# Attention stage of a hybrid decoder: the queries are projected first, projections run four steps further ahead, stored outputs return one transfer per step, the values' staging gets a second buffer, and chunk copies are placed behind the tiles turned on TensorE

## The chip, the cores and the metric

One Trainium2 chip, one of its NeuronCores. A core has five engines with a queue of instructions each, which meet only through semaphores: TensorE (PE, with weight loads shown apart as PEld), VectorE (DVE), ScalarE (ACT), GpSimd (POOL) and SyncE (SP), and 16 DMA engines that the queues of SP and POOL feed here. The metric is the device time of one execution in microseconds (us); several executions are summed up by their median.

## The reference

The whole trunk is one program: a recurrent layer, an attention layer, a dense feed-forward network behind each, with an RMS norm ahead of every part. The change touches the attention layer alone: 1024 positions, 16 heads of 64, causal, and instead of a softmax each weight is a share of what the later positions have left over.

```python
def stick_breaking_attention(x, w_qkv, w_o):
    qkv = jnp.einsum("bsd,de->bse", x, w_qkv).reshape(bsz, seq, 3, N_HEADS, HEAD_DIM)
    ...
        z = jnp.einsum("bhqd,bhkd->bhqk", qb, kb).astype(jnp.float32) * scale
        log_fail = jnp.where(strict, jax.nn.log_sigmoid(-z), 0.0)
        suffix = lax.cumsum(log_fail, axis=3, reverse=True) - log_fail
        weights = jnp.where(strict, jnp.exp(jax.nn.log_sigmoid(z) + suffix), 0.0)
        outs.append(jnp.einsum("bhqk,bhkd->bhqd", weights.astype(vb.dtype), vb))
    ...
    return jnp.einsum("bse,ed->bsd", o, w_o)
```

## The kernel before

Numbers that enter a matmul are split into a high and a low part, and a product is three matmuls (high by high, high by low, low by high: lines 143 to 145). Attention takes the 16 heads as eight pairs `q` = 0 to 7, each with two heads `hx`.

**Projections.** `qkv_steps(q)` projects queries, keys and values of a pair from the layer's input `xh`, `xl` (eight slices of 128 features, two halves `n` of 512 positions). One of its steps is three matmuls, one of its six groups (a projection of one half) is eight steps. After a group `evacuate` takes the result out of PSUM: queries and keys into `two` (high and low), from which `spread` sends them by DMA on POOL's queue into the tiles `q` (four transfers of 128 KB a half) and `kk` (four of 256 KB); values into `t` and from there, in two tasks a step apart, into `vx` (high by ACT, low by DVE), which two DMA transposes on SP's queue turn into `v`. `vx` has one buffer before. Of pair 0 the order is queries, keys, values, and of later pairs keys, queries, values (`kind`).

**The main loop.** It runs over steps `u`. A step computes the scores of one chunk (128 queries by up to 512 keys, `z_part`, L1682 and L1683), puts them through a sigmoid (ACT, L1695) and a running product (DVE, `scan`, L1702 and L1705), multiplies one finished tile of weights by the values (`av_part`, L1750), does two steps of projections (`fill`), one task of the list `later` and the tasks of the list `soon` that are due. 24 steps make a pair. Chunks run ten steps ahead of the multiplication by the values. The projections stand further ahead by `AHEAD` of their own steps.

**Two ways to turn weights.** Before they meet the values, weights must have keys on the partitions. Chunks on the diagonal are turned by PE itself (`t_part`, L1727), copied as `th` (ACT) and `tl` (DVE) by `t_split`. The four chunks of a head off the diagonal go through `turn_weights`: `wx` (high by ACT, L1712, low by DVE, L1713, three buffers) and a DMA transpose on SP's queue, `wt<-wx`. `av_part` reads `wt` at the steps with a remainder of 8 to 11 (first head) and 20 to 23 (second head) by 24; the four transposes of the first head are issued at steps -1 to 2, those of the second at 11 to 14. In a step, the copy of the chunk before stands ahead of `t_split`.

**Outputs.** A pair's output is added up by `gather`, `add_v` (L1766, on POOL, for pair 7 on DVE) and `parts`. The outputs of pairs 0 to 5 and the first half of pair 6 can't stay on the chip, since `xh` and `xl` are still read; `store` sends them to DRAM (`odh`, `odl`, 256 KB each), and when the last values are projected `bring_back` loads them into `xh` and `xl`, whose tiles bear names of earlier use in the profile (`vh`, `vl`, `xg`). There are 26 such transfers on POOL's queue, 12 issued at step 163 and 14 at step 168. `out_fill` puts the first matmuls of the output projection (`ob`) into the last steps; `amount` lists how many at which step, counted from 168.

The lists `soon` and `later` and the loop itself write the order of every engine's queue; nothing is reordered afterwards. A tile with several buffers waits, when it is written again, for the last readers of the buffer.

Of the kernel before, what the change touches and what calls it, by code (L numbers as in the profile page):

```python
# [10 lines left out]
BF16 = mybir.dt.bfloat16  # L11
F16 = mybir.dt.float16
# [5 lines left out]
P = 128  # L18
S = 1024
D = 1024  # L20
# [14 lines left out]
def trunk(  # L35
# [93 lines left out]
    def cols(w, c0, n=P):  # L129
        return w[:, c0 : c0 + n].rearrange("(k p) c -> p k c", p=P)  # L130
# [1357 lines left out]
    with ExitStack() as st:  # L1488
# [21 lines left out]
        later, soon, raws, sv, av_ = [], [], {}, {}, {}  # L1510

        def bring_back(*which):
            for q, n in which:
                nc.gpsimd.dma_start(f32(xh[q][n]), od[q, n][0])
                nc.gpsimd.dma_start(f32(xl[q][n]), od[q, n][1])


        def kind(q, i):
            return i if q == 0 else (1, 0, 2)[i]

        def stage(task, steps=1):
            soon.append([steps, task])

        def load_link(i):
            q, which = divmod(i, 3)
            if q < NP:
                raws[i] = load_raw(cols(w_qkv, kind(q, which) * D + q * P), (ND,))
            else:
                mix[0].load(which)

        def column_norms(raw, q):
            sq = ap.tile([P, ND, P], BF16, tag="sq", name="sq", bufs=1)
            r3 = raw.rearrange("p (k c) -> p k c", k=ND)
# [38 lines left out]
        def qkv_steps(q):  # L1572
            for which in range(3):
# [12 lines left out]
                for n in range(NH):  # L1586
                    pool, tag = (psZ, "z") if (q, which) == (0, 0) else (psQ, "qk")
                    ps = pool.tile([P, NB], F32, tag=tag, name="qk_ps")
                    for i, k in enumerate(ks):
                        mm3(ps, w[0][:, k], w[1][:, k], xh[k][n], xl[k][n], i == 0, i == ND - 1)  # L1590
                        if i < ND - 1:
                            yield
                    ev = evacuate(q, kind(q, which), n, ps)
                    next(ev)
# [4 lines left out]
        def evacuate(q, which, n, ps):  # L1599
            full = lambda tag, m: [ap.tile([P, m, S], F32R, tag=tag, name=tag, bufs=4 if m == 1 else 3) for _ in range(2)]  # L1600
            cs = slice(n * NB, (n + 1) * NB)
            if which == 2:
# [6 lines left out]
                nc.vector.scalar_tensor_tensor(after, ps, f32(sv[q]), rbc[n], op0=ALU.mult, op1=ALU.mult)  # L1609
                yield  # L1610
                nc.vector.tensor_sub(t, VT[q][:, cs], after)
                vx = ap.tile([P, 4, 2, P], F16, tag="vx", name="vx", bufs=1)
                t3 = t.rearrange("p (b c) -> p b c", b=4)

                def low():
# [3 lines left out]
                    for hx, a in enumerate((top, bot)):  # L1619
# [4 lines left out]
                        )  # L1624
                    if q == NP - 1:
                        back = [(p, n) for p in range(NP - 2)]
                        stage(lambda: bring_back(*([(NP - 2, 0)] * n + back)), 1 + n)

                def high():
# [112 lines left out]
        def av_part(tht, q, hx, G, kb, first, last):  # L1742
# [21 lines left out]
            def add_v():  # L1764
                eng = nc.vector if q == NP - 1 else nc.gpsimd
                eng.tensor_add(oo[q, G], oo[q, G], VT[q][:, G * NB + 1 : (G + 1) * NB + 1])  # L1766
# [27 lines left out]
        units = [u for q, hx in heads for u in unit_list(q, hx)]  # L1794
        LEAD, AHEAD = 10, 4

# [26 lines left out]
        with tc.manual_schedule(engines={E.PE, E.Activation, E.DVE, E.Pool, E.SP}):  # L1823
# [30 lines left out]
            last_two, out_work = len(units) - 2 * 12, out_fill()  # L1854
            amount = {x: 2 for x in (-1, 0, 1, 9, 10, 11, 12)}
            amount.update({x: 1 for x in range(14, 21)})
            c = 0
            for u in range(-LEAD, len(units)):
                some = chunks[c : c + 1]
                c += 1  # L1860
                if u < -2:
                    for _ in range(2):
                        next(fill, None)
                due()
                for a in some:
                    z_rest(z_part(*a), *a)
                    if u % 2 or u < -2:
                        scan(*a)
                while turning:
                    turn_weights(*turning.pop(0))  # L1870
                for a in some:
                    if not a[-1]:
                        turning.append(a)
                if u % 2 == 0 and u >= 0:
                    av_part(ready.pop(u, None), *units[u])
                if u % 2 == 0 and 0 <= u + 2 < len(units):
                    two = {x: t_part(*units[x]) for x in (u + 2, u + 3) if x % 12 < 8}
                    for x, tp in two.items():
                        ready[x] = t_split(tp, *units[x])
                if u % 2 == 0 and u >= -2:  # L1880
                    for a in some:
                        scan(*a)
# [67 lines left out]
```

## Time and profile before

| what | value |
|---|---|
| time, median of 3 runs | 2190.91 us (2189.57 to 2195.8) |
| the profiled execution | 2187.32 us, its span 2185.5 us |
| granted TensorE clock, mean | 0.992 |
| busy of the span: PE, DVE, ACT, POOL | 98%, 81%, 52%, 11% |
| attention stage | from about 955 to 1465 us of the span |
| wt<-wx transposes | 64, median 4.3 us from issue to landing |

The profile lists instructions by line, engine and tiles (out<-in, buffer numbers left out). "Idle before" is the time that an engine stood still ahead of an instruction, and the name behind it is what ended last of what it waited for. A wait names only the last link: where ACT keeps PE waiting, ACT's own waits must be looked up.

### The profile page before, as it was taken

Reading aid. Unit: us, or ns where it says so; the run is one execution under the profiler, and the core shown is the slowest. Engines: PE = TensorE matmul, PEld = TensorE weight load, DVE = VectorE, ACT = ScalarE, POOL = GpSimd, SP = SyncE. Lnnn points to the kernel's source line nnn. Section 1 sums busy time; section 2 is a strip of 40 time slices with the busy share of each in tenths; the row PEclk is TensorE's granted clock in tenths of the full one; section 3 lists DMA queues with packets and bytes.
Section 4 is the critical chain, followed back from the end, with each engine's and each line's share of the span. In section 5 each row is a group of like instructions: output and inputs, shape, how many; then the busy total and the mean of one; then the engine's idle time right before and its main releaser. Section 6 shows DMA issues by size and latency. Waiting matters only on the chain.

```text
span 2185.5 us, 28142 instructions
## 1 busy us (share of the span) xinstructions
PE 2132.9 (98%) x10158; PEld 1743.8 (80%) x10158; DVE 1780.7 (81%) x2607; ACT 1130.6 (52%) x1838; POOL 233.7 (11%) x282
## 2 busy tenths in 40 slices
PE   8999999999999999999999999779999999999998
PEld 7888888888888888887777777558888888888887
DVE  7888778888888887877888888766888888888886
ACT  6577445444444544655565565443544444454556
POOL 1222020000000000012223322411000000000002
PEclk9999999999999999999999999889999999999999
DMA  7111422344446864446777766984133444587452
GB/s 233 49 49 39 164 89 71 102 136 149 145 157 201 275 206 122 147 141 126 146 154 147 145 134 136 206 180 133 56 105 120 154 144 151 170 277 238 138 152 92
DMA packets 380843, 315.46 MB, mean 144 GB/s; under 512 B 101272, under 2 KB 296992, under 8 KB 380704
## 3 DMA queue, kind: packets, MB, share of 16 engines
q1 hardware_dynamic: 368192, 274.60, 42.7%
q0 software_dynamic: 12352, 38.81, 7.9%
q8 instruction: 79, 1.29, 0.2%
q14 instruction: 60, 0.49, 0.1%
q10 hardware_dynamic: 160, 0.27, 0.0%
HBM read 184.09 MB, written 83.36 MB: 122 GB/s over the span
## 4 chain that ended last, share of the span: by engine, by line
PE 86%; DMA 5%; DVE 5%; ACT 2%; issue 2%; SPq 0%; DVEq 0%; ACTq 0%
PE p_ps L143 17%; PE p_ps L144 17%; PE p_ps L145 17%; DMA wt<-wx 3%; PE a_ps L144 3%; PE a_ps L145 3%; PE a_ps L143 3%; PE ob_ps L143 2%; PE ob_ps L145 2%; PE ob_ps L144 2%; PE qk_ps L143 2%; PE qk_ps L145 2%; PE qk_ps L144 2%; PE av_ps L1750 2%; DMA v<-vx 2%
## 5 line engine op out<-in xcount | busy, mean ns | idle before, releaser
L143 PE MATMUL p_ps<-vh,wbh 128*128 128x512 f32 x524 | 204.9, 391 | 0.0
L144 PE MATMUL p_ps<-vl,wbh 128*128 128x512 f32 x524 | 204.5, 390 | 0.0
L145 PE MATMUL p_ps<-vh,wbl 128*128 128x512 f32 x524 | 204.0, 389 | 0.2 <-DVE wbl L726 0.2
L143 PE MATMUL p_ps<-vh,wch 128*128 128x512 f32 x524 | 204.1, 390 | 0.0
L145 PE MATMUL p_ps<-vh,wcl 128*128 128x512 f32 x524 | 204.1, 389 | 0.0
L144 PE MATMUL p_ps<-vl,wch 128*128 128x512 f32 x524 | 203.9, 389 | 0.0
L722 ACT CAST wbh<-sb 128x1024 fp32r<-128x1024 f32 (+2 forms) x69 | 69.6, 1009 | 192.6 <-DVE sb L702 192.6
L1695 ACT ACTIVATE w<-z_ps,rs 128x128 f32<-128x128 f32 (+1 forms) x192 | 111.1, 581 | 94.9 <-PE z_ps L1683 93.6
L145 PE MATMUL p_ps<-vh,wal 128*128 128x512 f32 x396 | 154.1, 389 | 0.0
L143 PE MATMUL p_ps<-vh,wah 128*128 128x512 f32 x396 | 154.0, 389 | 0.0
L144 PE MATMUL p_ps<-vl,wah 128*128 128x512 f32 x396 | 154.0, 389 | 0.0
L1702 DVE TENSOR_TENSOR_SCAN w<-w,unit 128x128 f32<-128x128 f32 (+3 forms) x128 | 104.2, 820 | 39.6 <-ACT w L1695 39.4
L218 POOL TENSOR_TENSOR acc<-acc,rbc 128x512 f32<-128x512 f32 x30 | 40.6, 1353 | 771.5 <-ACT rbc L217 771.5
L145 PEld LDWEIGHTS p_ps<-vh,wbl 128*128 128x128 f32 x524 | 98.4, 188 | 21.6 <-DVE wbl L726 0.7
L145 PEld LDWEIGHTS p_ps<-vh,wcl 128*128 128x128 f32 x524 | 98.4, 188 | 21.1 <-DVE wcl L736 0.6
L144 PEld LDWEIGHTS p_ps<-vl,wch 128*128 128x128 f32 x524 | 98.3, 188 | 20.4
L143 PEld LDWEIGHTS p_ps<-vh,wch 128*128 128x128 f32 x524 | 98.3, 188 | 20.5 <-ACT tb L1181 0.2
L143 PEld LDWEIGHTS p_ps<-vh,wbh 128*128 128x128 f32 x524 | 98.6, 188 | 19.9 <-ACT U L1181 0.4
L144 PEld LDWEIGHTS p_ps<-vl,wbh 128*128 128x128 f32 x524 | 98.6, 188 | 18.5
L143 PE MATMUL qk_ps<-vh,whi 128*128 128x512 f32 x264 | 112.0, 424 | 0.0
L145 PE MATMUL qk_ps<-vh,wlo 128*128 128x512 f32 x264 | 103.6, 392 | 0.0
L144 PE MATMUL qk_ps<-vl,whi 128*128 128x512 f32 x264 | 103.4, 392 | 0.0
(411 smaller groups left out, 5968.0 us busy)
## 6 DMA issues: line engine op xcount, KB each, us to landing
raw<-in_ffn_w_in SPq DMA_DIRECT2D x88, 512.0 KB, 4.0
vl<-pd SPq DMA_DIRECT2D x128, 256.0 KB, 3.7
pd<-U SPq DMA_DIRECT2D x90, 256.0 KB, 2.3
kk<-two POOLq DMA_DIRECT2D x64, 256.0 KB, 6.8
raw<-in_ffn_w_out SPq DMA_DIRECT2D x56, 256.0 KB, 3.7
raw<-in_attn_w_qkv SPq DMA_DIRECT2D x24, 512.0 KB, 6.7
h<-hd SPq DMA_DIRECT2D x32, 256.0 KB, 5.1
hd<-h SPq DMA_DIRECT2D x32, 256.0 KB, 2.0
```

The source lines that it names most:

```text
L143: nc.tensor.matmul(ps, lhsT=wh, rhs=mh, start=first, stop=False, **kw)
L144: nc.tensor.matmul(ps, lhsT=wh, rhs=ml, start=False, stop=False, **kw)
L145: nc.tensor.matmul(ps, lhsT=wl, rhs=mh, start=False, stop=last, **kw)
L218: (eng or nc.gpsimd).tensor_add(acc[n], acc[n], sq)
L722: nc.scalar.copy(self.full(self.wb), self.full(self.sb))
L1695: nc.scalar.activation(F, ps[:, 0:n], AF.Sigmoid, scale=rs[:, j : j + 1])
L1702: nc.vector.tensor_tensor_scan(rev, rev, unit[:, NB - n :][:, ::-1], 0.0, op0=ALU.mult, op1=ALU.add)
L1750: nc.tensor.matmul(ps[:, q0:], lhsT=VV[q][:, hx, kb], rhs=t[:, q0:], start=first and x == 0, stop=last and x == 1)
```

## The change

Pairs after the first take queries, keys, values like pair 0 (`kind` is gone). `AHEAD` is 8 instead of 4: projections stand four of their steps, two steps `u`, earlier. The tile `sq` of the column norms and `vx` share one tag with two buffers, instead of one buffer each. `bring_back` only fills a list, `back`; each step issues one transfer of it, from step 168 two. `add_v` runs on DVE for pairs 6 and 7. `turn_weights` of the chunk before now stands behind the chunk's running product in odd steps, and in even steps behind `t_split`. The output projection's matmuls start at step 163 with one a step, instead of two a step at 167 to 169.

```diff
@@ the lists and the projections
+        back = []
         def bring_back(*which):
             for q, n in which:
-                nc.gpsimd.dma_start(f32(xh[q][n]), od[q, n][0])
-                nc.gpsimd.dma_start(f32(xl[q][n]), od[q, n][1])
-        def kind(q, i):
-            return i if q == 0 else (1, 0, 2)[i]
+                for x, dst in enumerate((xh, xl)):
+                    back.append((f32(dst[q][n]), od[q, n][x]))
...
-                raws[i] = load_raw(cols(w_qkv, kind(q, which) * D + q * P), (ND,))
+                raws[i] = load_raw(cols(w_qkv, which * D + q * P), (ND,))
...
-            sq = ap.tile([P, ND, P], BF16, tag="sq", name="sq", bufs=1)
+            sq = ap.tile([P, ND, P], BF16, tag="vx", name="sq", bufs=2)
...
-                    ev = evacuate(q, kind(q, which), n, ps)
+                    ev = evacuate(q, which, n, ps)
@@ evacuate, values
+                if q == NP - 1:
+                    bring_back(*([(NP - 2, 0)] * n), *((p, n) for p in range(NP - 2)))
                 nc.vector.tensor_sub(t, VT[q][:, cs], after)
-                vx = ap.tile([P, 4, 2, P], F16, tag="vx", name="vx", bufs=1)
+                vx = ap.tile([P, 4, 2, P], F16, tag="vx", name="vx", bufs=2)
...
-                    if q == NP - 1:
-                        back = [(p, n) for p in range(NP - 2)]
-                        stage(lambda: bring_back(*([(NP - 2, 0)] * n + back)), 1 + n)
@@ outputs
-                eng = nc.vector if q == NP - 1 else nc.gpsimd
+                eng = nc.vector if q >= NP - 2 else nc.gpsimd
@@ the main loop
-        LEAD, AHEAD = 10, 4
+        LEAD, AHEAD = 10, 8
...
-            amount = {x: 2 for x in (-1, 0, 1, 9, 10, 11, 12)}
-            amount.update({x: 1 for x in range(14, 21)})
+            amount = {x: 2 for x in (9, 10, 11, 12)}
+            amount.update({x: 1 for x in (*range(-5, 1), *range(14, 21))})
+            def turn(some):
+                for a in some:
+                    turn_weights(*a)
...
                 due()
+                for _ in range(1 if u < last_two else 2):
+                    if back:
+                        nc.gpsimd.dma_start(*back.pop(0))
                 for a in some:
                     z_rest(z_part(*a), *a)
                     if u % 2 or u < -2:
                         scan(*a)
-                while turning:
-                    turn_weights(*turning.pop(0))
-                for a in some:
-                    if not a[-1]:
-                        turning.append(a)
+                now, turning = turning, [a for a in some if not a[-1]]
+                if u % 2 or u < -2:
+                    turn(now)
                 if u % 2 == 0 and u >= 0:
                     av_part(ready.pop(u, None), *units[u])
                 if u % 2 == 0 and 0 <= u + 2 < len(units):
...
                 if u % 2 == 0 and u >= -2:
+                    turn(now)
                     for a in some:
                         scan(*a)
```

POOL's queue at the end of attention before: the addition for pair 6, first half (L1766), the first of the 12 transfers that come back, the two stores of pair 6 (L1783, L1784), the first of the 14 others, and behind the last of these the addition for pair 6's second half.

```order
L1766 TENSOR_TENSOR oo<-oo,vt 128x512
L1514 DMA vh_3_2532<-odh_0_7885 128x512
L1515 DMA vl_3_2533<-odl_0_7886 128x512
...
L1515 DMA xg_6482<-odl_0_7896 128x512
L1783 DMA odh_0_7897<-oh 128x512
L1784 DMA odl_0_7898<-oo 128x512
L1514 DMA vh_1_2548<-odh_0_7897 128x512
...
L1515 DMA xg_6484<-odl_1_7910 128x512
L1766 TENSOR_TENSOR oo<-oo,vt 128x512
```

The same place of the changed kernel, from the spread of pair 7's keys on (L1641, eight transfers):

```order
L1641 DMA kk<-two 64x2x512 x8
L1548 TENSOR_SCALAR sv<-nh 128x1
L1549 TENSOR_SCALAR av<-nh 128x1
L1604 MEMSET vt 128x1
L1869 DMA vh_3_2532<-odh_0_7885 128x512
...
L1869 DMA vl_3_2541<-odl_0_7890 128x512
L1780 DMA odh_0_7897<-oh 128x512
L1781 DMA odl_0_7898<-oo 128x512
L1869 DMA xg_7655<-odh_0_7891 128x512
...
L1869 DMA xg_6484<-odl_1_7910 128x512
```

Six transfers now stand ahead of pair 6's stores and twenty behind them, and no addition stands among them.

SP's queue over one head pair before: the values' transposes, the four chunk transposes of the first head, a load of projection weights, then the second head.

```order
L1620 DMA_TRANSPOSE v<-vx 128x8x64 x2
L1716 DMA_TRANSPOSE wt<-wx 128x8x128 x4
L116 DMA raw<-in_attn_w_qkv 128x8x128
L1716 DMA_TRANSPOSE wt<-wx 128x8x128
L116 DMA raw<-in_attn_w_qkv 128x8x128
L1716 DMA_TRANSPOSE wt<-wx 128x8x128 x3
```

And in the changed kernel:

```order
L1621 DMA_TRANSPOSE v<-vx 128x8x64 x2
L1713 DMA_TRANSPOSE wt<-wx 128x8x128 x3
L116 DMA raw<-in_attn_w_qkv 128x8x128
L1713 DMA_TRANSPOSE wt<-wx 128x8x128
L116 DMA raw<-in_attn_w_qkv 128x8x128
L1713 DMA_TRANSPOSE wt<-wx 128x8x128 x4
```

The weights' load has moved from behind the fourth transpose of the first head to ahead of it, and the second load from behind the second head's first transpose to ahead of it.

## The prediction

> **What bounds the kernel now.** I went from the page to the waits of TensorE (PE) in the two parts of the attention stage, then to the timelines of the engines it waits for. On the page PE is busy for nearly the whole span; outside attention it hardly idles, so what this change can win lies in PE's idle time inside attention. First, who ended the idle time of PE while the eight head pairs run (960 to 1400 us), then in the last stretch (1400 to 1470 us): total, times, longest.
>
> ```profile
> PE av_ps L1750 <- DMA wt<-wx: 9.5, 6, 2.9
> PE av_ps L1750 <- DVE tl L1737: 4.0, 7, 0.6
> PE av_ps L1750 <- ACT th L1736: 2.7, 6, 1.4
> PE av_ps L1750 <- issue: 1.4, 1, 1.4
> ```
> ```profile
> PE z_ps L1682 <- ACT w L1695: 19.7, 2, 10.6
> PE av_ps L1750 <- DMA wt<-wx: 2.0, 1, 2.0
> PE av_ps L1750 <- DVE tl L1737: 0.2, 1, 0.2
> ```
>
> So the pairs lose 9.5 + 4.0 + 2.7 + 1.4 = 17.6 us, a bit at a time, and the last stretch loses 21.9 us, nearly all of it in two holes. ScalarE (ACT) causes both holes, but only by waiting itself; its own waits name two different culprits.
>
> ```profile
> ACT vx L1630 <- DMA v<-vx: 26.0, 8, 10.6
> ...
> ACT vh L1773 <- POOL oo L1766: 9.6, 1, 9.6
> ```
>
> The timelines of ACT, PE and GpSimd (POOL) in the last stretch put them in order (start, length, engine, line, in brackets the idle time before it):
>
> ```profile
> 1411.67 0.63 ACT L1630 ACTIVATE vx<-t 128x512 f16<-128x512 f32 x1 [10.56 <-DMA v<-vx]
> ...
> 1436.07 0.72 ACT L1773 ACTIVATE vh<-oo,av 128x512 fp32r<-128x512 f32 x1 [9.62 <-POOL oo L1766]
> ```
> ```profile
> 1399.39 0.50 PE L1682 MATMUL z_ps<-kk,q 128*128 128x512 f32 x1
> ...
> 1412.93 0.80 PE L1682 MATMUL z_ps<-kk,q 128*128 128x512 f32 x1 [10.59 <-ACT w L1695]
> ...
> 1437.20 0.80 PE L1682 MATMUL z_ps<-kk,q 128*128 128x512 f32 x1 [9.13 <-ACT w L1695]
> ...
> 1443.22 1.03 PE L1750 MATMUL av_ps<-wt,v 128*128 128x512 f16 x2 [1.96 <-DMA wt<-wx]
> ```
> ```profile
> 1434.93 1.10 POOL L1766 TENSOR_TENSOR oo<-oo,vt 128x512 f32<-128x512 f32 x1
> ```
>
> Hole one: `vx`, the values' staging, has one buffer, and its transposes are slow, because the first flood of bring-back transfers runs beside them. Hole two: the addition L1766 for pair 6 stands on POOL behind the issues of the second flood. Around them the granted clock falls (columns: window, its length, busy us of PE, PEld, DVE, ACT, POOL with counts, granted clock, DMA share, GB/s):
>
> ```profile
> 1402.00:1419.00 17.00, 6.41 (x22) 4.43 (x21) 9.08 (x13) 5.19 (x10) 6.51 (x13) 0.60 0.93 228
> 1419.00:1429.00 10.00, 8.82 (x52) 6.30 (x50) 7.45 (x12) 4.51 (x10) 4.46 (x9) 1.00 1.12 213
> 1429.00:1451.00 22.00, 11.84 (x36) 7.03 (x37) 10.73 (x13) 8.52 (x16) 2.98 (x4) 0.61 0.79 128
> ```
>
> PE's 6.41 + 11.84 = 18.25 us at about 0.61 would be some 7 us less at full clock. All that the last stretch can give is therefore 21.9 + 7 = 29 us. The same rows say that the DMA engines were the busy ones there.
>
> **The change, part by part.** *Values' staging doubled.* `vx` and the squares `sq` now share two buffers, no memory added. The wait of 26.0 us on ACT goes: 10.6 of it is hole one, the other 15.4 are 2.2 us in each of seven pairs, hidden from PE but making ACT and VectorE (DVE) late a few steps ahead of the `th`, `tl` waits. I find no late user of the shared slots: the squares are summed two steps before values arrive.
>
> *Addition of pair 6 on DVE.* One addition moves past the POOL queue, and hole two's cause goes. It costs DVE two additions, and I also need DVE's other prices, from its groups by shape (count, busy us, mean ns, idle before):
>
> ```profile
> L1705 DVE TENSOR_TENSOR_SCAN w<-w,w 128x512 f32<-128x512 f32 x64 | 87.4, 1366 | 9.1 <-ACT w L1695 9.1
> L1713 DVE TENSOR_TENSOR wx<-w,wx 128x512 f16<-128x512 f32 x64 | 44.3, 694 | 7.6 <-ACT wx L1712 5.5
> ...
> L1737 DVE TENSOR_TENSOR tl<-wt_ps,th 128x512 f16<-128x512 f32 x32 | 22.0, 687 | 15.7 <-ACT th L1736 15.5
> ...
> L1766 DVE TENSOR_TENSOR oo<-oo,vt 128x512 f32<-128x512 f32 x2 | 1.4, 694 | 0.1
> ```
>
> Two times 0.69 us, beside DMA waits: nothing on the path.
>
> *Outputs back one transfer per step.* The name promises more than the order gives. POOL does not know steps; only what stands between the issues holds them back, and that is the two stores of pair 6 alone. So six transfers go about six steps sooner, and the other twenty follow the stores in one run. This is the term I distrust. Floods slow the transposes, as the issues of two windows show, 1398 to 1416 us (the single `wt` left when the flood had passed) and 1416 to 1443 us (median us to landing):
>
> ```profile
> v<-vx SPq DMA_TRANSPOSE x2, 9.3
> wt<-wx SPq DMA_TRANSPOSE x1, 3.1
> ```
> ```profile
> wt<-wx SPq DMA_TRANSPOSE x4, 11.0
> ```
>
> In the changed kernel the last transposes of `vx` and the four of pair 7's first head start right with the run of twenty. Bytes: 22 transfers of 0.262 MB, four `wx` of 0.262 and two `vx` of 0.131, 7.1 MB. At 228, 213 or (mean of the three windows, weighted by length) 180 GB/s that is 31, 33 or 39 us. The stores belong to the step whose score matmul started at 1399.39, so the flood starts near 1400.4 and ends at 1431 to 1440, 1433 by the middle rate. PE must wait for the last of these transposes, as it did until 1443.22. Gain of the last stretch: 3 to 12 us by this sum, 29 us if the transposes are not held up after all. I take 9, since the rows of floods are nearest, and the clock will fall again after such a hole. What is late next is ACT: `wx` has three buffers, so the fourth copy waits for the first transpose; this hole lies inside the flood and is not added.
>
> The Trainium skill, "DMA: Bandwidth & Descriptors", section "Queues, rings and completion order", says that each DMA engine takes turns between its queues packet by packet. By that a transpose in small packets gets little until nearly all of the large ones are through; the sum with that rule would be about 15 us of gain in all instead of 20. The trace agrees in kind (3.1 us against 11.0).
>
> *Queries first, four steps ahead, copies behind the tiles.* One pair's `wt` wait, in the timelines: the issues of SyncE and of POOL (its second store follows these rows), the PE wait they end in, and the same wait one pair earlier.
>
> ```profile
> 1294.34 13.47 SPq L1716 DMA_TRANSPOSE wt<-wx  x4
> 1307.86 0.88 SPq L116 DMA_DIRECT2D raw<-in_attn_w_qkv  x1
> ```
> ```profile
> 1299.14 2.38 POOL L1644 DMA_DIRECT2D kk<-two  x4
> 1303.18 0.57 POOL L1783 DMA_DIRECT2D odh<-oh  x1 [1.66 <-ACT oh L1773]
> ```
> ```profile
> 1312.17 0.59 PE L1750 MATMUL av_ps<-wt,v 128*128 128x512 f16 x2 [1.41 <-issue]
> ```
> ```profile
> 1254.29 0.59 PE L1750 MATMUL av_ps<-wt,v 128*128 128x512 f16 x2 [1.25 <-DMA wt<-wx]
> ```
>
> Beside the four transposes ran 1 MB of keys and 0.5 MB of stores. Now it is 0.5 MB of queries, the same stores, and 0.5 MB of weights, since the load that stood behind the fourth transpose stands ahead of it on SyncE. The bytes stay equal. What improves is when the chunks reach the queue: the 2.2 us of ACT's wait are gone, and one product and one subtraction per pair leave these steps on DVE. Against it the fourth copy stands behind two `tl` of up to 0.69 us and their casts. Between 0 and 2 us sooner; the `wt` waits (9.5 + 1.4 us) average 1.6 us a pair, and I take 6 us off them in all. Of the 6.7 us on `th` and `tl`, 5 go, since both their causes are eased and they now stand ahead of the copies. Bounds: nothing, or all 17.6. The four steps ahead move 12 matmuls from the end to the front: PE work either way, nothing. The two output steps a step become one a step, six steps ahead of the old place; their data arrive with the flood, which is counted.
>
> Sum: 11 + 9 = 20 us. The profiled execution took 2187.3 us (span 2185.5), so it would take 2167; the median of the runs shown is 3.6 us above it, 2190.9, so I predict 2171 for the median.
>
> **The rivals.** *The last stretch clears.* If two buffers and the six early transfers keep the transposes ahead of the flood, all 29 us go: 2190.9 - 11 - 29 = 2151. For it: both holes have causes that the change names. Against it: 7.1 MB at the rates above.
>
> *ACT is held for the flood.* If no transpose passes until the 22 transfers are done (5.8 MB at 213 GB/s, 27 us, until 1427.5), ACT's fourth copy and the eight steps behind it come after that. These hold at least eight scans of up to 1.37 us and copies of 0.69, about 12 us, so the last stretch ends near 1439.5 and gains 4: 2176. The rule named above leads here.
>
> *Keys come late: slower.* The keys' second half, twice the bytes of the queries it replaces, now leaves six steps ahead of its first reader. A step is (1312.17 - 1254.29) / 24 = 2.41 us; six are 14.5, less 2.38 for the four issues, 12.1 us to land. Median landing, 1030 to 1395 us:
>
> ```profile
> kk<-two POOLq DMA_DIRECT2D x48, 256.0 KB, 7.0
> ```
>
> That leaves 5 us, so it decides only from a landing of 12 us on. At 15 us each of seven pairs waits 3 us, 21 in all; with 9 won at the end and nothing in the pairs the time is 2203.
>
> *It does not do what it says.* The holes are only renamed (ACT waits for `wx` instead of `vx`), the flood ends near 1440, and the pair waits move to the other head: 2187.
>
> **How the numbers follow.** Forecast 2171, chance 0.55, its own range 2163 to 2181. Clears 0.15; ACT held 0.10; nothing 0.10; late keys 0.10. A measurement of this kernel tells 0.3% (6.6 us) from no change, so faster means under 2184.3: 0.55 + 0.15 + 0.09 = 0.79; within 0.11; slower 0.10. The range reaches from the clearing case, 2148, to 2186, which leaves out the late keys and part of the others.
>
> **What would show it.** Right: no wait of `vx` on its transposes; PE's `th` and `tl` waits under 2 us in all; one or two new holes on PE between the stores of pair 6 and the last `wt`, with ACT waiting for `wt<-wx`; `wt` landing 10 us and more there. Wrong: PE without holes after the pairs (then 2151), or waits of z_ps on `kk` in every pair (then slower), or `wt` waits at the second head of each pair, which would mean that the keys took the queries' place in the way.

## The result, and the profile after

The changed kernel takes 2214.7 us (median of four runs, 2211.7 to 2216.6), the kernel before 2192.1 in runs beside it: a ratio of 1.0101, 95% interval 1.0081 to 1.012. The forecast was 2171, faster. By the medians the change made it 22.6 us slower, and the range (2148 to 2186) does not hold the time. The two profiled executions, from which all that follows is read, lie 28.3 us apart (2215.64 and 2187.32), so their differences come out somewhat larger than those of the medians. Lines of the changed kernel are about three less than before (L1713 the transpose `wt<-wx`, L1709 and L1710 the copies `wx`, L1679 the first score matmul, L1747 the multiplication by the values, L1641 the keys' transfers, L1780 and L1781 the stores, L1869 the bring-backs).

The loss lies in two stretches. The first score matmul of step 158, where the last stretch begins, starts at 1407.7 us instead of 1386.9, and from there to the last `av_ps` it takes 85.9 us instead of 78.6: 20.8 us lost in the pairs and 7.3 in the last stretch. The 720 us behind attention are the same in both.

PE's longer waits in the changed kernel (total, times, longest), first from 960 to 1421 us, then from 1421 to 1495:

```profile
PE z_ps L1679 <- ACT w L1692: 16.1, 8, 3.1
PE av_ps L1747 <- DMA wt<-wx: 10.1, 5, 2.6
PE av_ps L1747 <- issue: 2.3, 1, 2.3
```
```profile
PE z_ps L1679 <- ACT w L1692: 17.7, 2, 14.0
PE av_ps L1747 <- DMA wt<-wx: 5.4, 2, 4.3
```

The `th` and `tl` waits of the pairs are gone, as forecast. The `wt` waits are not smaller: 10.1 + 2.3 us, against 9.5 + 1.4 before. New is a wait of the scores on ACT: one in each pair, and 14 us in the last stretch. Two of ACT's own waits, 960 to 1495 us:

```profile
ACT wx L1709 <- DMA wt<-wx: 59.1, 8, 19.7
ACT vx L1627 <- DVE t L1612: 26.7, 8, 4.7
```

The first did not occur before, and it is the one that PE ends up waiting for. Before, ACT waited 26.0 us for `vx` on its transposes; that wait is gone, but at the same copy ACT now waits as long for DVE's subtraction `t`. That second wait is as long with AHEAD 9 below (32.9 us), where PE stands still in no pair, so it does no harm there. Six pairs of each kernel as windows (window, length, busy us of PE, PEld, DVE, ACT, POOL, granted clock, DMA share, GB/s), the kernel before first:

```profile
1003.00:1349.00 346.00, 332.62 (x1728) 250.91 (x1727) 295.58 (x440) 204.27 (x406) 95.37 (x147) 1.00 0.73 144
```
```profile
1004.80:1373.20 368.40, 343.37 (x1730) 257.64 (x1728) 295.79 (x443) 207.45 (x407) 89.93 (x147) 0.97 0.74 136
```

The same matmuls keep PE busy 10.8 us longer, at a mean granted clock of 0.97, and PE idles 25.0 us instead of 13.4. About half of the loss in these pairs is waiting, the other half a lower granted clock. The clock does not fall behind every wait. From 960 to 1400 us PE has twelve waits of 0.9 us and more. Behind seven of them (2.07 to 3.06 us) the clock was 0.83 over the ten us from the start of the wait, behind the other five (1.45 to 2.52 us) it was 1.00. Of the seven, three are waits of `z_ps` on ACT and four are waits of the first head on `wt`. In the kernel before, the clock stayed at 1.00 behind all seven such waits (1.25 to 2.88 us); why it does not there stays open. Two windows around the wait of 2.8 us that ends at 1356.02 us:

```profile
1344.00:1354.00 10.00, 9.26 (x51) 6.96 (x49) 6.93 (x10) 3.40 (x7) 1.58 (x4) 1.00 1.14 134
1354.00:1364.00 10.00, 7.98 (x33) 5.94 (x34) 8.10 (x14) 5.14 (x12) 1.09 (x1) 0.83 0.63 136
```

One place where the scores wait, in the timelines of POOL, SyncE, ACT and PE of the changed kernel (start, length, engine, line; in brackets the idle time before it). It is the second head of a pair:

```profile
1280.07 2.33 POOL L1641 DMA_DIRECT2D kk<-two  x4 [12.53 <-ACT whi L1558]
```
```profile
1281.26 13.72 SPq L1713 DMA_TRANSPOSE wt<-wx  x4
```
```profile
1281.26 0.63 ACT L1709 CAST wx<-w 128x512 f16<-128x512 f32 x1
...
1283.89 0.62 ACT L1709 CAST wx<-w 128x512 f16<-128x512 f32 x1 [0.41 <-DVE w L1702]
...
1292.38 0.62 ACT L1709 CAST wx<-w 128x512 f16<-128x512 f32 x1 [5.99 <-DMA wt<-wx]
...
1293.94 0.50 PE L1679 MATMUL z_ps<-kk,q 128*128 128x512 f32 x1 [2.52 <-ACT w L1692]
```

The second half of the keys, four transfers of 256 KB, leaves at 1280.07, and in the middle of it the head's first transpose, at 1281.26. ACT is ready for the head's fourth copy at 1292.38 - 5.99 = 1286.39, that is 5.1 us behind that issue, but all three `wx` buffers are taken until the first transpose has landed, 5.99 us later. The sigmoids stand behind that copy on ACT, the scores find no free PSUM bank, and PE stops. The row of issues for 1276 to 1294 us gives the landings (count, KB each, median us):

```profile
q0 software_dynamic: 320, 1.05, 39.2%
q1 hardware_dynamic: 3168, 0.79, 34.1%
...
kk<-two POOLq DMA_DIRECT2D x4, 256.0 KB, 5.5
wt<-wx SPq DMA_TRANSPOSE x4, 10.2
```

The last stretch shows the same thing with the bring-backs in place of the keys (POOL, SyncE, ACT, PE):

```profile
1424.87 0.54 POOL L1780 DMA_DIRECT2D odh<-oh  x1 [12.56 <-ACT oh L1770]
...
1456.95 0.55 POOL L1869 DMA_DIRECT2D xg<-odl  x1 [0.77 <-issue]
```
```profile
1433.44 39.05 SPq L1713 DMA_TRANSPOSE wt<-wx  x5
```
```profile
1456.88 0.62 ACT L1709 CAST wx<-w 128x512 f16<-128x512 f32 x1 [19.70 <-DMA wt<-wx]
```
```profile
1457.92 0.79 PE L1679 MATMUL z_ps<-kk,q 128*128 128x512 f32 x1 [13.97 <-ACT w L1692]
```

Between the issues of the first store and of the last of the twenty bring-backs lie 32 us. The forecast's 31 to 39 us stood for something longer, the time until the last transpose is through: PE's last wait on these transposes ends at 1471.02 us, 46 us behind the first store. What the forecast left out is that ACT stands for 19.70 us in between, so that the fourth copy, and with it the last transpose, starts late.

### The profile page after: what moved, and what is told of

The parts are those of the page before. It is cut to its first block, busy times and chain, and to the rows that moved or that the text cites. A ratio compares the mean times of both kernels' runs of the same rounds, so it can differ in the third digit from the quotient of the medians.

```text
span 2213.5 us, 28166 instructions
## 1 busy us (share of the span) xinstructions
PE 2146.3 (97%) x10158; PEld 1752.4 (79%) x10158; DVE 1781.0 (80%) x2609; ACT 1133.3 (51%) x1838; POOL 225.5 (10%) x280
## 4 chain that ended last, share of the span: by engine, by line
PE 89%; DMA 7%; DVE 1%; issue 1%; ACT 1%; POOL 0%; DVEq 0%; ACTq 0%; POOLq 0%
PE p_ps L143 17%; PE p_ps L144 17%; PE p_ps L145 17%; DMA wt<-wx 7%; PE qk_ps L143 3%; PE qk_ps L144 3%; PE qk_ps L145 3%; PE a_ps L144 3%; PE a_ps L145 3%; PE a_ps L143 3%; PE ob_ps L143 2%; PE ob_ps L145 2%; PE ob_ps L144 2%; PE av_ps L1747 2%; PE z_ps L1679 1%
## 5 line engine op out<-in xcount | busy, mean ns | idle before, releaser
L1679 PE MATMUL z_ps<-kk,q 128*128 128x256 f32 (+1 forms) x192 | 83.1, 433 | 33.7 <-ACT w L1692 33.7
```

The lines of the kernel that those rows point to most:

```text
L1679: nc.tensor.matmul(ps[:, 0 : c1 - c0], lhsT=lhsT, rhs=KK[q][hx][:, 0, c0:c1], start=True, stop=False)
```

## The experiments

The theory: *the place of the keys*. With queries first and AHEAD 8, the keys' halves leave at steps 8 and 12 of a pair (2 and 6 before), and the second half meets the first transpose of the second head (in the timelines above it is issued 1.2 us behind the first of these transfers). That transpose then holds the ring of three `wx` buffers past the fourth copy. Rivals: the copies' new place behind the tiles does it; standing further ahead costs by itself; or the flood of the last stretch is the whole matter.

The table gives, for every kernel that ran, the steps at which the keys' halves leave, the time and its ratio to the kernel before with its interval, and from the traces the mean length of a pair (first scores of steps 0 and 144, a sixth of the difference) and of the last stretch (first scores of step 158 to the last `av_ps`). Profiles are single executions, some of them a few us under their kernel's median; the one of *keys alone* is its fastest of seven, 9 us under.

| kernel | keys | time, us | ratio to before | pair | last stretch |
|---|---|---|---|---|---|
| before | 2, 6 | 2192.1 | 1 | 57.7 | 78.6 |
| changed | 8, 12 | 2214.7 | 1.0101 [1.0081, 1.012] | 61.4 | 85.9 |
| four `wx` buffers | 8, 12 | 2195.1 | 1.0015 [1.0004, 1.0026] | 58.1 | 85.3 |
| half the keys' bytes | 8, 12 | 2180.0 | 0.9943 [0.9922, 0.9964] | 56.4 | 77.4 |
| keys first | 0, 4 | 2231.7 | 1.0188 [1.0167, 1.0209] | 63.0 | 76.8 |
| copies ahead of tiles | 8, 12 | 2231.6 | 1.0186 [1.0166, 1.0206] | 63.5 | 87.5 |
| old place, rest of the change | 2, 6 | 2185.7 | 0.9978 [0.9959, 0.9996] | 58.0 | 78.7 |
| AHEAD 12 | 6, 10 | 2164.9 | 0.9886 [0.986, 0.9912] | 55.2 | 66.4 |
| before, new place alone | 6, 10 | 2170.5 | 0.9908 [0.9886, 0.9929] | 55.3 | 75.3 |
| AHEAD 12, copies ahead | 6, 10 | 2168.2 | 0.9901 [0.9879, 0.9924] | 55.3 | 72.2 |
| AHEAD 9 | 7, 11 | 2164.9 | 0.9882 [0.9863, 0.9901] | 55.0 | 72.1 |
| keys alone one step earlier | 7, 11 | 2187.0 | 0.9968 [0.9951, 0.9986] | 56.8 | 75.4 |
| queries alone one step earlier | 8, 12 | 2212.3 | 1.009 [1.0059, 1.0122] | 61.4 | 85.6 |
| before, two holes closed | 2, 6 | 2183.6 | 0.9961 [0.9946, 0.9976] | 58.2 | 77.6 |
| changed, held POOL | 8, 12 | 2218.9 | 1.0122 [1.0102, 1.0143] | 62.2 | 85.3 |
| AHEAD 12, four `wx` | 6, 10 | 2160.4 | 0.9865 [0.9842, 0.9889] | 55.2 | 63.1 |
| AHEAD 9, four `wx` | 7, 11 | 2162.7 | 0.9859 [0.9833, 0.9885] | 55.1 | 70.4 |
| AHEAD 9, held POOL | 7, 11 | 2152.4 | 0.981 [0.9792, 0.9828] | 55.0 | 60.9 |

### Is it the ring, and is it the bytes?

**Four `wx` buffers** in the changed kernel (`t` gives up one for them).

```diff
-            wx = ap.tile([P, 4, 2, P], F16, tag="wx", name="wx", bufs=3)
+            wx = ap.tile([P, 4, 2, P], F16, tag="wx", name="wx", bufs=4)
-                t = ap.tile([P, NB], F32, tag="t", name="t", bufs=2)
+                t = ap.tile([P, NB], F32, tag="t", name="t", bufs=1)
```

> Changed kernel with a fourth buffer for wx, paid for by giving t one buffer instead of two. Theory (the ring of three wx buffers: keys and returning outputs slow a transpose, ACT's fourth copy waits for it, PE waits for ACT): ACT's 59 us of waiting for wt<-wx fall under 5, PE's 33.7 us on z_ps fall under 5, and the time falls by 20 to 30 us, to 2185 to 2195, with the wt waits of about 2 us a pair left. Rival (the place of the copies behind the turned tiles makes the transposes late): PE's waits turn up elsewhere and the time stays at 2210 to 2217.

2195.1 us, 20 less than the changed kernel. PE's waits from 1010 to 1360 us, where the changed kernel had six of `z_ps`:

```profile
PE av_ps L1747 <- DMA wt<-wx: 9.3, 4, 3.3
PE av_ps L1747 <- issue: 2.9, 1, 2.9
```

No `z_ps` wait is left in the pairs; the `wt` waits of the first head stay. In the last stretch (1400 to 1475 us) nothing is won: PE now waits for the transposes themselves.

```profile
PE av_ps L1747 <- DMA wt<-wx: 25.0, 2, 22.8
```

So the ring carries the scores' wait in the pairs; in the last stretch it only decides which instruction shows it.

**Half the keys' bytes**, everything else in its place. The kernel leaves out the low parts of the keys; the scores use the high part twice, so that PE has the same matmuls.

```diff
-                            nc.gpsimd.dma_start(f32(KK[q][hx])[half_, :, cs], f32(two)[a])
+                            nc.gpsimd.dma_start(f32(KK[q][hx])[half_, 0, cs], f32(two)[a, 0])
...
-            nc.tensor.matmul(ps[:, 0 : c1 - c0], lhsT=lhsT, rhs=KK[q][hx][:, 1, c0:c1], start=False, stop=True)
+            nc.tensor.matmul(ps[:, 0 : c1 - c0], lhsT=lhsT, rhs=KK[q][hx][:, 0, c0:c1], start=False, stop=True)
```

> The changed kernel with the keys' transfers cut to the high parts (128 KB instead of 256 KB each, same count, same places; scores use the high part twice, so the result differs). Theory (bytes beside the transposes): the second head's first transpose lands well before the fourth copy asks for its buffer, so the z_ps waits in the pairs go; the first head's wt waits of some 2 us a pair stay, since no keys run there; 2197 us, 2190 to 2203. Rival (the transposes are slow because of something else in these steps: the count of transfers, the issue order, the weights' load): no change, 2212 to 2217.

2180.0 us, 10 below the expected range. The `z_ps` waits are gone from the pairs (1010 to 1360 us), part of the `wt` waits stays:

```profile
PE av_ps L1747 <- DMA wt<-wx: 6.6, 4, 2.5
PE av_ps L1747 <- issue: 1.0, 1, 1.0
```

The second head's transposes land in 3.2 us instead of 10.2 (median of four, 1252 to 1272 us):

```profile
wt<-wx SPq DMA_TRANSPOSE x4, 3.2
```

With the same count of transfers, issues and order, halving the keys' bytes ends the scores' waits, so it is the bytes. By the Trainium skill ("DMA: Bandwidth & Descriptors", section "Queues, rings and completion order") each DMA engine takes turns between its queues packet by packet. The turns themselves show in no run here. The rows of issues above fit them: 320 packets on POOL's queue held 1.05 MB, 3168 on SyncE's 0.79 MB, so that by this rule a turn would move, as an estimate, some 13 times as many bytes of keys as of a transpose.

### Which edit brings it?

**Keys first** again, AHEAD left at 8 (`kind` is used at the same two places as before).

```diff
+        def kind(q, i):
+            return i if q == 0 else (1, 0, 2)[i]
```

> Changed kernel, but pairs after the first project keys, then queries, then values, as before. Theory: the keys no longer run beside the second head's transposes, so PE's z_ps waits in the pairs (six of 1.6 to 3.1 us, 14.5 in all) go and the time falls by 12 to 20 us, to 2195 to 2203; the hole of 14 us near the end stays, since there the returning outputs hold the transposes. Rival (copies behind the tiles, or four steps ahead): z_ps waits in the pairs stay, 2210 to 2217.

2231.7 us: a miss, by 30 us and in sign. The keys then leave at steps 0 and 4, beside the transposes of the *first* head, which are issued at steps -1 to 2. PE's waits from 1010 to 1360 us:

```profile
PE av_ps L1750 <- DMA wt<-wx: 28.8, 5, 9.4
PE av_ps L1750 <- issue: 9.6, 1, 9.6
```

The collision was not taken away but moved to the other head, whose fourth transpose lands late for its reader at step 8. What decides is the step at which the keys leave; the order matters only in that it sets this step.

**Copies ahead of the tiles**, as before the change, in even steps.

```diff
-                if u % 2 or u < -2:
-                    turn(now)
+                turn(now)
...
-                    turn(now)
```

> Changed kernel, but the copy of the chunk before stands ahead of t_split again in even steps. Theory: the copies leave about 1 us sooner, the fourth copy meets its held buffer all the more, 2209 to 2217 and ACT's waits for wt<-wx within 15% of 59 us. Rival (the place of the copies is the cause): 2190 to 2198, ACT's waits for wt<-wx under 20 us.

2231.6 us, 17 more than the changed kernel, and more than expected. With the copy ahead of `t_split`, a held copy holds `th` as well (1010 to 1360 us):

```profile
PE av_ps L1747 <- ACT th L1733: 23.4, 5, 5.6
```

So the copies' new place behind the tiles is no cause of the loss; it makes the same hold cheaper.

**Old place, rest of the change**: keys first and AHEAD 4.

```diff
-        LEAD, AHEAD = 10, 8
+        LEAD, AHEAD = 10, 4
+            return i if q == 0 else (1, 0, 2)[i]
-            amount = {x: 2 for x in (9, 10, 11, 12)}
+            amount = {x: 2 for x in (-1, 0, 1, 9, 10, 11, 12)}
```

> The changed kernel with keys first and AHEAD 4 as before the change (output projection's first steps placed as before); doubled staging, copies behind tiles, one bring-back per step and the addition on VectorE stay. Theory: the keys leave at steps 2 and 6 between the heads' transposes, so the 21 us that the pairs lost come back and the th and tl waits are gone as well; the last stretch keeps its loss of 7 us; 2196 us, 2190 to 2201. Rival (copies behind the tiles or the doubled staging cost in the pairs): 2203 and more, with pairs longer than 59 us.

2185.7 us: the pairs are as long as before the change (58.0), in spite of doubled staging and copies behind the tiles. PE's waits from 1010 to 1360 us:

```profile
PE av_ps L1750 <- DMA wt<-wx: 10.9, 5, 2.6
PE av_ps L1750 <- issue: 2.9, 1, 2.9
```

The `th` and `tl` waits (4.8 us in the same window of the kernel before) are gone, and the `wt` waits have grown by what they left (13.8 us against 9.1): nothing of the 11 us that the forecast had taken off the pairs comes from these edits. The last stretch did not keep its loss (78.7 us), against the expectation: that loss came with the place as well.

### How far must the keys move?

**AHEAD 12** in the changed kernel: keys at steps 6 and 10.

```diff
-        LEAD, AHEAD = 10, 8
+        LEAD, AHEAD = 10, 12
```

> The changed kernel with AHEAD 12 instead of 8, so that the keys' two halves leave at about steps 6 and 10 of a pair instead of 8 and 12. Theory (the keys' bytes beside the second head's four transposes, issued at steps 11 to 14, hold the ring of three wx buffers and with it ACT): half of the keys' bytes are through before the first of these transposes, the others still run beside it, so PE's waits of z_ps on ACT in the pairs (14.5 us in six pairs) at least halve; 2203 us, 2195 to 2210. Rival (standing further ahead costs by itself, whatever the keys meet): 2215 or more, with the z_ps waits as long as before.

2164.9 us, 50 less than the changed kernel and 27 less than before. No wait of PE is left in the pairs, not even the `wt` waits that the kernel before had. A miss in size: the theory had the two collide in part still.

**AHEAD 9**: keys at steps 7 and 11.

```diff
-        LEAD, AHEAD = 10, 8
+        LEAD, AHEAD = 10, 9
```

> The changed kernel with AHEAD 9, which puts the keys' halves at steps 7 and 11, half way between the changed kernel (8 and 12) and AHEAD 12 (6 and 10). Theory: the second half now leaves with the second head's first transpose (step 11) instead of one step behind it, so its bytes still run beside the first three; the hold of ACT shortens by about a step (2.4 us) in each of six pairs: z_ps waits fall from 14.5 to under 5 us, 2195 us, 2180 to 2208. Rival (only a place that clears the transposes helps, the nearer the worse): 2212 or more.

2164.9 us as well, a miss: the expectation had the keys still beside three of the transposes, and 2180 at the least. One step of AHEAD is worth all of the 50 us: not a slope, an edge. The six pairs and the same place as above, in the kernel with AHEAD 9:

```profile
1007.50:1337.70 330.20, 330.20 (x1730) 250.79 (x1728) 290.91 (x443) 209.60 (x407) 87.25 (x147) 1.00 0.73 152
```
```profile
1251.83 2.33 POOL L1641 DMA_DIRECT2D kk<-two  x4 [4.27 <-ACT w L1692]
```
```profile
1256.47 10.60 SPq L1713 DMA_TRANSPOSE wt<-wx  x4
...
1263.42 0.64 ACT L1709 CAST wx<-w 128x512 f16<-128x512 f32 x1
```
```profile
kk<-two POOLq DMA_DIRECT2D x4, 256.0 KB, 4.3
wt<-wx SPq DMA_TRANSPOSE x4, 3.1
```

PE is busy for all 330.2 us, at full clock. The keys' issues end at 1254.16, 2.3 us ahead of the first transpose, which has 7.0 us until the fourth copy at 1263.42, and the four land in 3.1 us instead of 10.2. The slack fits the edge in the scores' waits: 5.1 us from the first issue to the fourth copy when the keys leave at the same time, against 10 us of landing; 7.0 against 3.1 when they leave a step earlier.

**Keys alone** and **queries alone** one step earlier, in the changed kernel, since AHEAD moves both.

```diff
@@ keys
-                def high():
-                    nc.scalar.copy(two[:, 0], t)
-                    stage(low)
-                stage(high)
+                nc.scalar.copy(two[:, 0], t)
+                stage(low)
@@ queries (the other kernel)
-                stage(spread)
+                stage(spread) if which else spread()
```

> The changed kernel with the keys alone one step earlier (their high part is copied in the step of the product instead of the next): keys at steps 7 and 11, queries left at -2 and 2. Theory (the keys' second half must have left before the second head's first transpose): PE's z_ps waits in the pairs go, the first head's wt waits of 2.1 us a pair stay, since queries and stores still run there; with the half clock behind each wait 4 of the 6.4 us a pair come back, 2188 us, 2178 to 2197. Rival (the queries' place makes the larger part): 2203 or more, z_ps waits still there.

> The changed kernel with the queries alone about one step earlier (their transfers are issued right behind the subtraction instead of a step later); keys left at steps 8 and 12. Theory: the first head's wt waits (12.4 us in six pairs) shrink, the z_ps waits stay; 2202 us, 2194 to 2210. Rival (queries' place makes the larger part): under 2190.

The keys alone give 2187.0 us, as the theory said, the queries alone 2212.3, next to nothing. PE's waits from 1010 to 1360 us, keys alone first (L1744 is the multiplication by the values there), then queries alone:

```profile
PE av_ps L1744 <- DMA wt<-wx: 6.9, 4, 2.6
PE av_ps L1744 <- issue: 1.8, 1, 1.8
```
```profile
PE z_ps L1679 <- ACT w L1692: 16.1, 6, 3.7
PE av_ps L1747 <- DMA wt<-wx: 7.3, 4, 2.4
PE av_ps L1747 <- issue: 1.7, 1, 1.7
```

The keys' step makes the `z_ps` waits, and it alone is worth 28 of the 50 us. The other 22 come with what else AHEAD moves; the queries alone bring next to none of it, and no run takes the rest apart. What makes the first head's `wt` waits stays open: they went with AHEAD 9 and 12, which move queries, values and weight loads too, but not with the queries alone, where the expectation (2194 to 2210) missed. So the four dips of the clock behind these waits in the changed kernel are not explained either.

**The new place without the other edits**: the kernel before with queries first and AHEAD 12, its two bursts of bring-backs kept at their steps.

```diff
-            return i if q == 0 else (1, 0, 2)[i]
+            return i
-                        stage(lambda: bring_back(*([(NP - 2, 0)] * n + back)), 1 + n)
+                        stage(lambda: bring_back(*([(NP - 2, 0)] * n + back)), 5 + n)
-        LEAD, AHEAD = 10, 4
+        LEAD, AHEAD = 10, 12
```

> The kernel before with queries first and AHEAD 12 alone (the two bursts of bring-back stay at steps 163 and 168; one vx buffer, copies ahead of the tiles, addition of pair 6 on GpSimd as before). Theory (the keys' place between the heads' transposes is what decides the pairs): most of the 18 us that the pairs gained at AHEAD 12 comes with this alone, and the last stretch keeps its holes; 2177 us, 2168 to 2184. Rival (the gain needs the other edits, copies behind tiles above all): 2187 or more.

2170.5 us, and pairs of 55.3 us with one `vx` buffer and copies ahead of the tiles: the place alone makes the pairs. **AHEAD 12 with the copies ahead of the tiles** (the edit shown above) agrees:

> The changed kernel with AHEAD 12 and the chunk copies ahead of the tiles in even steps, as before the change. At AHEAD 8 this edit cost 17 us, because a held copy then kept th as well. Theory: without a hold only the bare waits of th and tl come back (2.7 us of PE in seven pairs at the least, 6.7 as before the change); 2169 us, 2165 to 2174. Rival (copies behind the tiles are worth as much without a hold): 2180 or more.

2168.2 us, 3.3 more than AHEAD 12 with the copies behind (the intervals overlap), and the same pairs. What cost 17 us beside a held copy costs some 3 us, if anything, where none is held.

### The last stretch

**Before, with the two holes closed**: two `vx` buffers and the addition of pair 6 on DVE, nothing else.

```diff
-            sq = ap.tile([P, ND, P], BF16, tag="sq", name="sq", bufs=1)
+            sq = ap.tile([P, ND, P], BF16, tag="vx", name="sq", bufs=2)
-                eng = nc.vector if q == NP - 1 else nc.gpsimd
+                eng = nc.vector if q >= NP - 2 else nc.gpsimd
```

> Kernel before, with only vx and sq in one ring of two buffers and the addition of pair 6 on DVE: the two edits that name the two holes. If the holes were those edits' alone: both go with the clock dips, 2160 to 2166. Theory (returning outputs saturate the DMA engines, the waiting moves to wx): ACT waits 8 to 15 us for wt<-wx behind the second batch of returning outputs, and the gain is 3 to 14 us, 2177 to 2188.

2183.6 us: 8.5 us by the medians, close to the 9 that the forecast took for it, although the last stretch of its one profile is only 1.0 us shorter; where the rest lies is open. The closeness says little for the forecast: both holes are gone, but one as long as both together stands in their place, on the transposes themselves (1380 to 1500 us).

```profile
PE av_ps L1750 <- DMA wt<-wx: 19.7, 1, 19.7
```

ACT waits only 4.5 us for `wt<-wx` in this kernel, where the expectation had 8 to 15.

**Four `wx` buffers with AHEAD 12, and with AHEAD 9** (the edits shown above):

> The changed kernel with AHEAD 12 and four wx buffers (t gets one for it). Theory: the pairs, which had no wait left on PE at AHEAD 12, stay at 55.3 us; only the last stretch, where the flood still holds the ring, may gain up to the 4.5 us of its z_ps waits; 2162 us, 2158 to 2167. Rival (the ring of three was the cause by itself, the keys' place a second one, and both add up): under 2155.

> The changed kernel with AHEAD 9 and four wx buffers. Theory: pairs at 55.0 us as with AHEAD 9 alone; in the last stretch ACT is no longer held (11 us), PE's hole of 8.7 us moves to the wait for the transposes themselves; 0 to 5 us less than AHEAD 9 alone: 2161 us, 2157 to 2166. Rival (the ring makes the last stretch's loss): 2153 or less.

2160.4 and 2162.7 us: 4.5 and 2.2 less than without, and the intervals overlap. Once the keys are out of the way, a fourth buffer is worth a few us at most.

**POOL held to the steps.** A small addition on the weights of the step's chunk stands ahead of its bring-backs on POOL, so that POOL cannot run ahead. First in the changed kernel alone:

```diff
+                if back and some:
+                    g = ap.tile([P, 1], F32, tag="gate", name="gate", bufs=2)
+                    q_, hx_, j_, ci_ = some[0][:4]
+                    nc.gpsimd.tensor_scalar_add(g, W[q_, hx_, j_, ci_][:, 0:1], 0.0)
                 for _ in range(1 if u < last_two else 2):
                     if back:
                         nc.gpsimd.dma_start(*back.pop(0))
```

> The changed kernel with a small GpSimd addition ahead of each step's bring-back, which reads the weights of the step's chunk: GpSimd then can't run ahead, and one transfer (two from step 168 on) really leaves per step. Theory for the last stretch (a flood of twenty transfers in one run holds the transposes, these the ring of wx, this ACT): transposes there land in 5 to 8 us instead of up to 30, PE's hole of 14 us shrinks under 4; 2204 us, 2199 to 2209. Rival (the bytes must pass in these steps anyway, or the output projection now waits for its inputs): 2212 to 2220.

2218.9 us: the rival was right here. The flood is gone (transposes of 1423 to 1465 us in the row below, 20.8 us in the changed kernel) and with it PE's hole of 14 us, but the output projection's first matmuls now wait for their inputs (second rows, 1400 to 1502 us):

```profile
wt<-wx SPq DMA_TRANSPOSE x5, 3.2
```
```profile
PE ob L143 <- DMA vh<-odh: 8.8, 4, 3.6
PE ob L143 <- DMA xg<-odh: 7.0, 2, 5.3
PE ob L144 <- DMA vl<-odl: 4.5, 3, 2.1
PE z_ps L1679 <- ACT w L1692: 2.6, 1, 2.6
```

Then with AHEAD 9, and with these matmuls at steps 172 to 174 instead of 163 to 168:

```diff
-            amount.update({x: 1 for x in (*range(-5, 1), *range(14, 21))})
+            amount = {x: 2 for x in (4, 5, 6, 9, 10, 11, 12)}
```

> The changed kernel with AHEAD 9, GpSimd held to the steps by a small addition on the step's weights ahead of its bring-backs, and the output projection's first six matmul groups at steps 172 to 174 instead of 163 to 168, when their inputs are there. Theory (the flood, not the ring, makes the last stretch's loss): the holes of 8.7 and 6.6 us shrink to under 4 in all and the output projection does not wait; the last stretch falls from 72 to 62 us: 2154 us, 2149 to 2160. Rival (the same bytes cost the same wherever they go): 2163 or more.

2152.4 us, the fastest of all: 0.981 of before, interval 0.9792 to 0.9828. The transposes of the last stretch in the changed kernel (1423 to 1465 us), with AHEAD 9 and with AHEAD 9 and POOL held (both 1383 to 1425 us):

```profile
wt<-wx SPq DMA_TRANSPOSE x5, 20.8
```
```profile
wt<-wx SPq DMA_TRANSPOSE x5, 10.0
```
```profile
wt<-wx SPq DMA_TRANSPOSE x8, 3.8
```

From 20.8 to 10.0 to 3.8 us, with the last stretch at 85.9, 72.1 and 60.9 us. With AHEAD 9 PE still had holes of 8.7 and 6.6 us there; now its longest wait is 3.7 us. The two edits went in together, and no run moves the output projection's matmuls alone; with AHEAD 9 these waited 0.8 us in all, so their move alone had little to win. It is the flood that makes the holes, and a step of a list is not a step in time until something makes the queue wait.

## Why the prediction was wrong, point by point

- **The step that failed is the pairs' term.** The prediction took 11 us off the pairs; they lost 21. It weighed the transfers beside the *first* head's transposes ("The bytes stay equal") and found them equal; the 6 us that it took off the waits there did not come, they are 12.4 us against 10.9. It did not follow the keys to where they went, beside the second head's transposes, though it named that as a sign ("`wt` waits at the second head of each pair").
- **The hold of ACT was seen and put in the wrong place.** "`wx` has three buffers, so the fourth copy waits for the first transpose; this hole lies inside the flood and is not added." The same sum in a pair could have shown it: the prediction had a row of transposes landing in 11.0 us beside other transfers, and in the changed kernel a slack of 5.1 us met a landing of 10.2.
- **The clock was left out of the pairs.** Half of the loss there (10.8 of 22.4 us in six pairs) is matmuls at a lower granted clock, behind seven waits of 2 to 3 us. Three of these are the keys' doing; the other four are the first head's, whose cause stays open.
- **Right:** the wait of `vx` on its transposes is gone, though ACT waits as long there for DVE; the `th` and `tl` waits of the pairs are gone too. But the gain of 5 us that this was to give is not there even with the old place of the keys (58.0 us a pair against 57.7).
- **The last stretch:** forecast 9 us shorter, it was 7.3 longer. The sum had PE free of the transposes some 33 us behind the first store; it was 46. It also counted two transposes of `vx` in the flood, and four ran there. "ACT is held for the flood" came true (19.70 us), with a price that the rival had set too low: it had the hold end 27 us behind the stores, and the fourth copy came 32 us behind the first store (1456.88 - 1424.87); and the same hold came in every pair as well, which the rival did not have.
- **The rival "Keys come late"** had the sign and nearly the size (2203), by another mechanism: no score waited for keys; the keys delayed the transposes, and these ACT. That its size came near is luck.
- **The range** was built on cases that all took the pairs for won or even, but for that one rival. Six pairs multiply any wait by six; a term that repeats needs the wider bound.

## What to carry to other kernels

When a transfer moves by some steps, list what it now leaves beside, for every ring and reader there, and compare the slack (from the first issue to the moment when its buffer is wanted again) with the landing beside that traffic, not alone. Such a place can be an edge and not a slope: here one step of AHEAD was worth 50 us, 28 of them by the keys alone, so neighbouring steps should be tried before an idea is given up. And a DMA queue that waits for nothing runs ahead of the steps that it is written in; spreading transfers takes a wait that spreads them, and readers that come late enough.

## What the runs showed of the hardware that was not expected

- Transposes of 256 KB landed in 3.1 us behind four transfers of 256 KB from POOL's queue and in 10.2 us (median) when issued among them, 20.8 in the flood.
- Behind seven of twelve waits of PE of 1.45 to 3.06 us the granted clock was 0.83 over the ten us from the start of the wait; behind the other five, the longest of 2.52 us, it was 1.00. In six pairs with such waits PE was busy 10.8 us longer for the same matmuls.
- With no wait at all, PE was busy for 330.20 of 330.20 us at a granted clock of 1.00: the floor of a pair with this work on PE is 55.0 us, 2.7 under the kernel before.
